# A hybrid decoder layer on one core: the first residual add through a re-ordered copy of the input, VectorE transposes and GpSimd adds

## The chip, the core and the metric

The kernel runs on one core of a Trainium2 chip. The metric is the device time of one execution in microseconds (us). The engines of the core are TensorE (PE in the profile, with its weight loads as PEld), VectorE (DVE), ScalarE (ACT), GpSimd (POOL) and SyncE (SP), which here only issues transfers. The transfers run on 16 DMA engines.

## What is computed

One layer of a decoder on 1024 prompt tokens and 8 sample tokens, with D_MODEL = 1024, all in float32. The core of the reference:

```python
h = rmsnorm(x, w['norm1_w'])
proj = h @ w['w_in']                 # 6672 columns for two head groups
...                                  # group A: 8 HGRN2 heads; group B: 16 Mamba-2 heads
x = x + jnp.concatenate([o_a, y], axis=-1) @ w['w_out']      # first residual
h = rmsnorm(x, w['norm2_w'])
gate, val = jnp.split(h @ w['w_up'], 2, axis=-1)
gate, buf_f_new = causal_dwconv(gate, buf_f, w['ffn_conv_w'], w['ffn_conv_b'])
x = x + (jax.nn.silu(gate) * val) @ w['w_down']
y = rmsnorm(x, final_norm_w)
```

It also returns the new states of both head groups and of the convolutions. The change concerns the term `x +` of the first residual.

## The kernel before, in words

**Layout.** Activations are kept transposed: features on the 128 partitions, tokens along the free dimension, 1024 prompt tokens and then the 8 samples (NT = 1032). The 1024 features are 8 row blocks (KT = 8, index m). Each float32 product is made of three matmuls of split operands: high by high, high by low, low by high.

**Stages.** The input is loaded token by token, normalized and transposed (`first_norm`, L106). Then the columns of w_in are worked off, 128 at a time (`in_job`, L290), with the SSM scan (`ssd`, L715) and the eight HGRN2 heads (`head`, L823) laid between them. The output projection follows in jobs of two row blocks (`out_job`, L1028): first the half of w_out that belongs to the SSM heads (r0 = 8 and 12), then the half of the HGRN heads (r0 = 0 and 4). Then come the second norm, the up projection (`ups`, L1341) and the down projection (`down`, L1399), and the final norm.

**The order of the work.** PE's instructions are in a schedule written by hand (L1107): the jobs' matmuls are a list of steps, `drive` (L266) takes a share of steps for each piece of a scan or head, and `spread` (L240) and `after` (L229) hang small pieces of other work on the count of steps. The other engines' instructions have no such fixed order: a scheduler places each of them on its engine's queue as its inputs, buffers and priority allow. `fetch` (L172) ties a load to the last weight load; a plain `SP.dma_start` isn't tied. Each engine works off its queue in order, SP too: a transfer that waits for a buffer holds up those behind it. Transfers on SP's queue share eight completion semaphores in turn, so each waits until the eighth before it is done.

**The first residual.** For a job with r0 = 8, `out_job` calls `residual_load` (L769) for its two row blocks: for block m it loads the input's columns of that block as xs, two tiles of [128 tokens x 4, 128 features] each holding 512 tokens, in pieces of 512 bytes, and the samples as xd. xs comes from the tag "d" with four buffers, which the broadcast values vb of the heads (L843) use too. After the matmuls ACT copies the sums to x (L1052), and `residual` (L779) is spread over the following steps, 8 apart: PE transposes xs in blocks of 128x128 against the identity into a PSUM bank xtp (L787), DVE adds the bank to x (L782); the samples go through a small transpose xtd (L791). Since x is kept in two halves of 516 tokens, the second 512 prompt tokens are added in pieces of 4 and 508 columns. Later jobs (r0 = 12, 0, 4) add their sums to x on DVE (L1054). Other lines that the prediction names: the split of the mixed activations `ml` (L1012), the scale steps of a head (L866, L867, L872), the masks (L891), the weight split `wl` (L192), the state update `Sh` (L846 to L849), and, in the SSM scan, ecs (L576), S (L581, L582), Cb (L644), Sd (L638 to L643), csb (L543).

Of the kernel before, what the change touches and what calls it, by code (L numbers as in the profile page):

```python
# [8 lines left out]
F32 = mybir.dt.float32  # L9
# [3 lines left out]
ALU = mybir.AluOpType  # L13
# [3 lines left out]
P = 128  # L17
DM = 1024
T = 1024
ND = 8  # L20
# [3 lines left out]
KT = DM // P  # L24
# [26 lines left out]
def hybrid_layer(  # L51
# [9 lines left out]
    V, A, G, PE, SP = nc.vector, nc.scalar, nc.gpsimd, nc.tensor, nc.sync  # L61
# [5 lines left out]
    dram = ctx.enter_context(tc.tile_pool(name="dscr", bufs=1, space=DRAM))  # L67
# [3 lines left out]
    def nm(s):  # L71
        cnt[0] += 1
        return f"{s}_{cnt[0]}"
# [8 lines left out]
    def tl(tag, name, dt=F32):  # L82
        w, n = TAGS[tag]
        return (work if tag in ("hT", "big", "e", "g") else tmp).tile([P, w], dt, tag=tag, bufs=n, name=nm(name))
# [4 lines left out]
    def bank(s, tag="mx"):  # L89
        return psmx.tile([P, 512], F32, tag=tag, bufs=NBANK[tag], name=nm(s))  # L90
# [65 lines left out]
    ident = keep.tile([P, P], F32, name="ident")  # L156
# [15 lines left out]
    def fetch(dst, src):  # L172

        with tc.issue_after(last_w[0].ins):
            SP.dma_start(dst, src)
# [50 lines left out]
    def job(name, load, run):  # L226
        jobs.append((name, load, run))

    def after(n, work):  # L229

        later.append([n, work])
# [8 lines left out]
    def spread(pieces, n, then=None):  # L240

        def go():
            if next(pieces, 0) is None:
                after(n, go)
            elif then is not None:
                then()
        go()
# [72 lines left out]
    def conv_state(src2d, nrow, ntile, out):  # L320
        def rows(j0):
            rt = half("rt")
            nj = min(4, ntile - j0)
            fetch(rt[:nrow, :nj * P], src2d[:, j0 * P:(j0 + nj) * P])
            return rt, nj

        nxt = rows(0)
        for j0 in range(0, ntile, 4):
            yield
            (rt, nj), nxt = nxt, rows(j0 + 4) if j0 + 4 < ntile else None  # L330
            ps = bank("cst", "nx")
            for j in range(nj):
                PE.transpose(ps[:, j * nrow:(j + 1) * nrow], rt[:nrow, j * P:(j + 1) * P], ident[:nrow, :nrow])
            V.tensor_copy(out[:, j0:j0 + nj, :], ps[:, :nj * nrow].rearrange("p (j r) -> p j r", r=nrow))
# [92 lines left out]
    for c, cs in enumerate(chunks):  # L427
        ps = psmm.tile([P, 512], F32, tag="mm", name=nm("dt"))
# [273 lines left out]
    def ssm_conv_state():  # L702
        for j0 in range(0, XT, 4):
            yield
            ps = bank("l11", "nx")
            for j in range(4):
                PE.transpose(ps[:11, j * P:(j + 1) * P], last11[:, j0 + j, :], ident)
            csr = keep.tile([16, 512], F32, tag="csr", bufs=1, name=nm("csr"))
            V.tensor_copy(csr[:11, :512], ps[:11, :])
            cl = slice(j0 * P, (j0 + 4) * P)  # L710
            SP.dma_start(cs_prompt[0, 0, :, cl], csr[0:3, :512])
            SP.dma_start(cs_sample[0, :, 2, cl], csr[3:11, :512])
        SP.dma_start(cs_sample[0, :, 0:2, :], state_conv_ssm[0, :, 1:3, :])
# [16 lines left out]
    def once(work):  # L730
        def run():
            work()
            return
            yield
        return run
# [30 lines left out]

    blk = [slice(i * P, (i + 1) * P) for i in range(4)]

    def residual_load(m):  # L769
        ms = slice(m * P, (m + 1) * P)  # L770
        xs = [tl("d", "xs")[:, :512] for _ in range(2)]
        xd = small.tile([ND, P], F32, tag="xd", name=nm("xd"))
        for i in range(2):
            fetch(xs[i].rearrange("p (i m) -> p i m", m=P),
                  x_prompt[0, i * 512:(i + 1) * 512, ms].rearrange("(i p) m -> p i m", p=P))
        fetch(xd, x_sample[:, 0, ms])
        return xs, xd

    def residual(out, xs, xd):  # L779

        def add(x_, ps):
            V.tensor_tensor(x_, x_, ps, op=ALU.add)  # L782

        for i0 in range(2):
            ps = bank("xtp")
            for i in range(4):
                PE.transpose(ps[:, blk[i]], xs[i0][:, blk[i]], ident)  # L787
            if i0 == 0:
                add(out[0][:, 0:512], ps)
                ps = bank("xtd", "nx")  # L790
                PE.transpose(ps[:, :ND], xd, ident[:ND, :ND])  # L791
                add(out[1][:, 508:516], ps[:, :ND])
            else:
                add(out[0][:, 512:516], ps[:, 0:4])
                add(out[1][:, 0:508], ps[:, 4:512])
            yield

    xh = [[None] * KT for _ in range(2)]
# [1 line left out]
    def head_in(h):  # L800
        t = {}

        def f_end():
            f, k = t["f"], tl("big", "k")
            A.activation(f[:, :NT], f[:, :NT], AF.Identity, bias=lbt[:, 0, h:h + 1], scale=lbt[:, 1, h:h + 1])
            V.tensor_scalar(k[:, :NT], f[:, :NT], -1.0, 1.0, op0=ALU.mult, op1=ALU.add)
            t["k"] = k

        for n, off, func in (("f", OFF_F, AF.Sigmoid), ("q", OFF_Q, AF.Silu), ("v", OFF_I, AF.Copy),
                             ("sg", OFF_G, AF.Silu)):  # L810
            def evict(c, cs, ps, n=n, func=func):
                A.activation(t[n][:, cs], ps, func)

            def begin(n=n):
                t[n] = tl("e" if h == 0 and n == "f" else "big", n)

            if h == H - 1 and n == "sg":
                in_job_last(f"{n}{h}", off + h * P, evict, begin)
            else:
                in_job(f"{n}{h}", off + h * P, evict, begin, f_end if n == "f" else None)  # L820
        return t
# [206 lines left out]
    def out_job(r0, m, halves=(0, 1), last=False):  # L1028
        def load():
            w = wload(w_out[0, r0 * P:(r0 + 4) * P, m * P:(m + 2) * P], 4, 2 * P,  # L1030
                      kept=(r0 // 4 * 4 + m // 2, halves[0]) if len(halves) == 1 else None)
            return w, [residual_load(m + i) for i in range(2)] if r0 == 8 else None
# [52 lines left out]
    def conv_states():  # L1085
        yield from ssm_conv_state()
        yield from conv_state(state_conv_ffn[0].rearrange("b r d -> (b r) d"), 16, FT, fbufT)
        yield
# [3 lines left out]
    heads[0] = head_in(0)  # L1092
    ssm_gate(1)
    heads[1] = head_in(1)
    job("conv", None, once(lambda: spread(conv_states(), 60)))
    for h in range(2, H):
        heads[h] = head_in(h)

# [256 lines left out]
    with tc.manual_schedule(engines={mybir.EngineType.PE}):  # L1355
# [43 lines left out]
        def down(w, kt, msl, acts, c):  # L1399
            q = quarters[c]  # L1400
            ps = psmm.tile([P, 512], F32, tag="mm", name=nm("dn"))[:, :q.stop - q.start]
            for k in range(kt):
                hi, lo = acts[k]
                wh, wl = w(k)
                mm(ps, wh[:, msl], hi[:, q], start=(k == 0), stop=False)
                mm(ps, wh[:, msl], lo[:, q], start=False, stop=False)
                mm(ps, wl[:, msl], hi[:, q], start=False, stop=(k == kt - 1))
                tick()
            return ps

        acts = [act_load(k) for k in range(RND)]
        for r0 in range(0, FT - RND, RND):
# [3 lines left out]
            for m in range(0, KT, 2):  # L1416
                wh, wl = wload(w_down[0, rows, m * P:(m + 2) * P], nk, 2 * P)
                for i in range(2):
# [3 lines left out]
                    for c, cs in enumerate(quarters):  # L1422
                        ps = down(lambda k: (wh[:, k, :], wl[:, k, :]), nk, slice(i * P, (i + 1) * P), acts, c)
# [14 lines left out]
    for c in (3, 0, 1, 2):  # L1438
        cs = quarters[c]
        for m in range(KT):  # L1440
            ps = down(lambda k: wd[k], nk, slice(m * P, (m + 1) * P), acts, c)
# [52 lines left out]
```

## Time and profile before

| | |
|---|---|
| three timed runs | 1771.92, 1772.98, 1773.81 us; median 1772.98 |
| the profiled execution | the page gives its span, 1770.0 us; no other time of it is given |
| ACT busy, DVE busy, POOL busy over the span | 822.8, 1121.0, 476.3 us |
| granted TensorE clock, mean | 0.996 |
| DMA | 190.76 MB in 220325 packets, 13644 of them under 512 bytes |
| PE transposes of the residual (xtp) | 64, first at 835.0 us, last at 925.5 us |
| loads of xs | 16 of 256 KB, first issued at 783.0 us, last at 911.9 us |

A line of a timeline has the start in us, the duration, the engine, the line of the kernel, the operation, the output and inputs by name, and the shape; "x4" joins four instructions in a row, and a bracket gives the time that the engine sat idle before it and what ended that. Matmuls overlap, so the distance of their starts says more than their durations. A line of a group has the count, the busy time in us and the mean in ns, and then the idle time before them. The column "PEclk" is the TensorE clock that was granted, as a share of the full one.

### The profile page before, as it was taken

To read this page: it belongs to the slowest core of one execution; us is meant where nothing else is said; L and a number is where in the kernel's file an instruction comes from. 1 tells how busy PE (TensorE), PEld (TensorE's weight loads), DVE (VectorE), ACT (ScalarE), POOL (GpSimd) and SP (SyncE) were. 2 spreads that over 40 slices of the span, in tenths; PEclk is the share of its full clock that TensorE was granted. 3 is DMA by queue.
4 is the path that set the end of the run, shared out by engine and by line. 5 is a ranking of instruction groups with operands and counts; after the bars stand their busy time and mean duration, and the time that the engine had idled before them with its cause. 6 is when DMAs were issued, how large, how long until landed. Compare 5 with 4: busy or idle time off the path is not lost. (4 is left out here: it accounts for less than half of the span.)

```text
span 1770.0 us, 38596 instructions
## 1 busy us (share of the span) xinstructions
PE 1720.0 (97%) x16143; PEld 1672.4 (94%) x16143; DVE 1121.0 (63%) x2021; ACT 822.8 (46%) x1472; POOL 476.3 (27%) x477
## 2 busy tenths in 40 slices
PE   7999899999999999999999999999999999999997
PEld 6998798999999999999899989999999999999997
DVE  6667966565554564567746688776666767444545
ACT  7677688454544555455423374343333434111114
POOL 2103331120110110111100355666666664000002
PEclk9999999999999999999999999999999999999999
DMA  4144635542222221234336742222222225422212
GB/s 155 40 127 126 183 99 149 177 136 96 75 83 58 85 75 51 77 97 139 115 108 204 243 128 73 72 84 83 86 73 73 82 82 213 152 85 78 92 61 97
DMA packets 220325, 190.76 MB, mean 108 GB/s; under 512 B 13644, under 2 KB 195414, under 8 KB 220134
## 3 DMA queue, kind: packets, MB, share of 16 engines
q1 hardware_dynamic: 219862, 188.19, 34.0%
q8 instruction: 127, 2.08, 0.5%
q14 instruction: 48, 0.39, 0.1%
q0 software_dynamic: 288, 0.10, 0.0%
HBM read 145.72 MB, written 42.71 MB: 106 GB/s over the span
## 5 line engine op out<-in xcount | busy, mean ns | idle before, releaser
L93 PE MATMUL mm<-hh,wh 128*128 128x344 f32 x1248 | 406.9, 327 | 0.6 <-ACT sz L672 0.6
L93 PE MATMUL mm<-hl,wh 128*128 128x344 f32 x1248 | 406.0, 326 | 0.0
L93 PE MATMUL mm<-hh,wl 128*128 128x344 f32 x1248 | 403.7, 324 | 0.0
L93 PEld LDWEIGHTS mm<-hh,wh 128*128 128x128 f32 x1248 | 236.4, 190 | 4.2 <-issue 2.0
L93 PEld LDWEIGHTS mm<-hl,wh 128*128 128x128 f32 x1248 | 236.6, 190 | 2.4 <-issue 0.9
L93 PEld LDWEIGHTS mm<-hh,wl 128*128 128x128 f32 x1248 | 236.5, 190 | 2.0 <-issue 1.2
L190 ACT CAST wh<-ws 128x1024 fp32r<-128x1024 f32 x96 | 100.5, 1047 | 237.4 <-PE dn L93 135.5
L93 PE MATMUL ub<-uh,wh 128*128 128x258 f32 x704 | 199.3, 283 | 3.1 <-DVE fext L1307 2.7
L93 PE MATMUL ub<-ul,wh 128*128 128x258 f32 x704 | 199.0, 283 | 0.0
L93 PE MATMUL ub<-uh,wl 128*128 128x258 f32 x704 | 198.7, 282 | 0.0
L93 PE MATMUL dn<-ah,wh 128*128 128x256 f32 (+1 forms) x640 | 181.2, 283 | 2.1 <-DVE x L1424 2.1
L93 PE MATMUL dn<-al,wh 128*128 128x256 f32 (+1 forms) x640 | 180.6, 282 | 0.0
L93 PE MATMUL dn<-ah,wl 128*128 128x256 f32 (+1 forms) x640 | 180.1, 281 | 0.0
L192 DVE TENSOR_TENSOR wl<-ws,wh 128x1024 fp32r<-128x1024 f32 x88 | 115.6, 1313 | 72.1 <-ACT wh L190 71.1
L93 PE MATMUL ua<-uh,wh 128*128 128x258 f32 x528 | 149.6, 283 | 1.9 <-DVE val L1319 1.2
L93 PE MATMUL mm<-mh,wh 128*128 128x258 f32 x512 | 146.5, 286 | 3.5 <-DVE x L1054 2.1
L93 PE MATMUL ua<-ul,wh 128*128 128x258 f32 x528 | 149.3, 283 | 0.0
L93 PE MATMUL ua<-uh,wl 128*128 128x258 f32 x528 | 148.3, 281 | 0.0
L93 PE MATMUL mm<-mh,wl 128*128 128x258 f32 x512 | 145.0, 283 | 0.9 <-issue 0.9
L93 PE MATMUL mm<-ml,wh 128*128 128x258 f32 x512 | 145.1, 283 | 0.7 <-DVE ml L1012 0.7
L93 PEld LDWEIGHTS ub<-uh,wh 128*128 128x128 f32 x704 | 132.9, 189 | 3.7 <-DVE fext L1307 2.9
L1257 DVE TENSOR_TENSOR wl<-wt,wh 128x512 fp32r<-128x512 f32 x88 | 90.1, 1043 | 70.0 <-ACT wh L1256 69.7
(355 smaller groups left out, 4070.0 us busy)
## 6 DMA issues: line engine op xcount, KB each, us to landing
ws<-in_w_in_dram SPq DMA_DIRECT2D x52, 512.0 KB
ws<-in_w_up_dram SPq DMA_DIRECT2D x44, 512.0 KB
ws<-in_w_out_dram SPq DMA_DIRECT2D x24, 512.0 KB
act_d<-val SPq DMA_DIRECT2D x22, 516.0 KB
al<-act_d SPq DMA_DIRECT2D x22, 516.0 KB
ws<-in_w_down_dram SPq DMA_DIRECT2D x22, 512.0 KB
ml<-mix_d SPq DMA_DIRECT2D x48, 172.0 KB
csb<-cs_d SPq DMA_DIRECT2D x32, 256.0 KB
```

What stands on the lines that cost most here:

```text
L93: PE.matmul(out, lhsT, rhs, start=start, stop=stop)
L190: A.copy(wh[:, :n], ws[:, :n])
L192: V.tensor_tensor(wl[:, :n], ws[:, :n], wh[:, :n].bitcast(F32), op=ALU.subtract)
L1257: V.tensor_tensor(lo[:, cs], sums[name], hi[:, cs].bitcast(F32), op=ALU.subtract)
```

## The change

The input is first copied within memory to a scratch tensor `xb_d` in which each block of 32 tokens by 32 features stands so that a transpose within 32x32 blocks gives the wanted layout: row 32a + j, columns 32b to 32b + 31 of xb_d[m] hold the 32 features of column group a of block m for the token 32b + j. 32 transfers make this copy, each with 1024 pieces of 128 bytes. They are issued by `token_blocks`, started after the convolution states and spread 40 steps apart. `residual_load` then reads whole rows of xb_d. In `residual`, DVE transposes xs in place, 128x512 at once and block by block, and POOL adds the result to x; PE's transposes of xs and the PSUM bank are gone. The samples keep PE's small transpose and DVE's add.

```diff
+    xb_d = dram.tile([KT, P, T], F32, name="xb_d")
+
+    def token_blocks():
+        for m in range(KT):
+            for a in range(4):
+                f0 = m * P + 32 * a
+                SP.dma_start(xb_d[m, 32 * a:32 * a + 32].rearrange("j (b i) -> j b i", i=32),
+                             x_prompt[0, :, f0:f0 + 32].rearrange("(b j) i -> j b i", j=32))
+                yield
+
     def residual_load(m):
...
         for i in range(2):
-            fetch(xs[i].rearrange("p (i m) -> p i m", m=P),
-                  x_prompt[0, i * 512:(i + 1) * 512, ms].rearrange("(i p) m -> p i m", p=P))
+            fetch(xs[i], xb_d[m][:, i * 512:(i + 1) * 512])
         fetch(xd, x_sample[:, 0, ms])
         return xs, xd
 
     def residual(out, xs, xd):
 
-        def add(x_, ps):
-            V.tensor_tensor(x_, x_, ps, op=ALU.add)
+        def add(x_, y_):
+            G.tensor_tensor(x_, x_, y_, op=ALU.add)
 
         for i0 in range(2):
-            ps = bank("xtp")
-            for i in range(4):
-                PE.transpose(ps[:, blk[i]], xs[i0][:, blk[i]], ident)
+            V.transpose(xs[i0], xs[i0])
             if i0 == 0:
-                add(out[0][:, 0:512], ps)
+                add(out[0][:, 0:512], xs[0])
                 ps = bank("xtd", "nx")
                 PE.transpose(ps[:, :ND], xd, ident[:ND, :ND])
-                add(out[1][:, 508:516], ps[:, :ND])
+                V.tensor_tensor(out[1][:, 508:516], out[1][:, 508:516], ps[:, :ND], op=ALU.add)
             else:
-                add(out[0][:, 512:516], ps[:, 0:4])
-                add(out[1][:, 0:508], ps[:, 4:512])
+                add(out[0][:, 512:516], xs[1][:, 0:4])
+                add(out[1][:, 0:508], xs[1][:, 4:512])
             yield
...
-    job("conv", None, once(lambda: spread(conv_states(), 60)))
+    job("conv", None, once(lambda: spread(conv_states(), 60, lambda: spread(token_blocks(), 40))))
```

## The prediction, made before the change was run

> **What bounds the kernel now.** I read the page first, then the busy time by stage, then who waits for whom.
>
> ```profile
> span 1770.0 us, 38596 instructions
> PE 1720.0 (97%) x16143; PEld 1672.4 (94%) x16143; DVE 1121.0 (63%) x2021; ACT 822.8 (46%) x1472; POOL 476.3 (27%) x477
> ```
>
> TensorE (PE) is busy 97% of the span, so a microsecond counts only if it is taken from PE or from a wait of PE. The next view gives the busy time of each engine in chosen stages (columns: stage, its length, PE, PEld, DVE, ACT, POOL, granted clock, DMA share, GB/s):
>
> ```profile
> 150.00:230.00 80.00, 70.51 (x481) 64.53 (x480) 69.60 (x117) 54.88 (x117) 26.72 (x24) 0.98 0.61 172
> 820.00:840.00 20.00, 19.00 (x376) 18.08 (x376) 19.76 (x38) 12.87 (x28) 3.86 (x3) 1.00 0.47 157
> 840.00:860.00 20.00, 17.18 (x298) 15.66 (x297) 17.82 (x31) 11.47 (x27) 4.61 (x4) 1.00 0.66 193
> 860.00:926.00 66.00, 65.75 (x544) 64.43 (x543) 29.73 (x65) 19.46 (x38) 2.85 (x2) 1.00 0.26 81
> ```
>
> Three places matter. From 860 to 926 us PE is full and DVE is half empty: PE binds. From 820 to 860 PE loses 1.00 + 2.82 us and DVE is busy 37.6 of 40: there DVE binds nearly as much as PE. From 150 to 230 us, far ahead of the residual, PE loses 9.5 us while DVE is at 87% and DMA at 0.61: a stage of short chains with no slack. Its largest waits of PE, and those of ACT behind transfers there (total, times, longest), are:
>
> ```profile
> PE xp L554 <- DVE ecs L576: 2.9, 2, 2.7
> PE yo L93 <- DVE S L582: 2.6, 1, 2.6
> PE sT L607 <- POOL Cb L644: 2.1, 1, 2.1
> ACT Sd L640 <- DMA Sd<-in_state_ssm_dram: 11.2, 4, 6.4
> ACT csb L543 <- DMA csb<-cs_d: 7.8, 4, 3.6
> ```
>
> **What leaves PE.** The order of PE's instructions is written by hand, and in the changed program it is the old one without 64 transposes of 128x128 (L787). What one costs is read from starts, not from durations, because matmuls overlap:
>
> ```profile
> 902.55 0.28 PE L93 MATMUL mm<-mh,wl 128*128 128x258 f32 x1
> 902.67 0.60 PE L787 MATMUL xtp<-ident,xs 128*128 128x128 f32 x4
> 903.20 0.22 PE L791 MATMUL xtd<-ident,xd 8*128 8x8 f32 x1
> 903.36 0.39 PE L93 MATMUL mm<-mh,wh 128*128 128x258 f32 x1
> ...
> 904.43 0.60 PE L787 MATMUL xtp<-ident,xs 128*128 128x128 f32 x4
> 904.79 0.37 PE L93 MATMUL mm<-mh,wl 128*128 128x258 f32 x1
> 904.99 0.28 PE L93 MATMUL mm<-mh,wh 128*128 128x258 f32 x1
> ```
>
> A matmul of this stream starts every 0.12 us (902.55 to 902.67). The second group of four delays its successor by 0.36 us, and the successor then takes 0.20 instead of 0.12 to the next start: 0.44 us. The first group takes 0.53 us to the start of the small transpose xtd, which stays; some of that is xtd's own start, so 0.36 to 0.53. I take 0.45 for each of the 16 groups: 7.2 us, between 6.4 and 7.8. Ten groups stand after 860 us, where PE binds: 4.5 us gained in full. Six stand between 835 and 860, where DVE is late too: of their 2.7 us I count 1.5. **PE: -6.0 us.**
>
> **What changes on DVE.** It loses 24 adds and gains 16 transposes of 128x512 in place:
>
> ```profile
> L782 DVE TENSOR_TENSOR x<-x,xtp 128x512 f32<-128x512 f32 x8 | 5.5, 684 | 22.9 <-PE xtp L787 22.9
> L782 DVE TENSOR_TENSOR x<-x,xtp 128x508 f32<-128x508 f32 x8 | 5.4, 675 | 0.0
> L782 DVE TENSOR_TENSOR x<-x,xtp 128x4 f32<-128x4 f32 x8 | 1.2, 153 | 3.2 <-PE xtp L787 3.1
> L609 DVE COPY so<-sT 128x512 f32<-128x512 f32 x2 | 1.4, 676 | 0.0
> L806 DVE TENSOR_SCALAR k<-f 128x1032 f32<-128x1032 f32 x8 | 5.6, 695 | 3.4 <-ACT f L805 3.4
> ```
>
> The adds are 12.1 us. No row shows a DVE transpose. The nearest is the copy of 128x512 at 0.68; L806 does 1032 elements in 0.695, so 0.35 us is the low end, and four passes of the copy, 2.7 us, the high one. I take 0.68: 16 x 0.68 = 10.9 us, 1.2 less than the adds. [...] The first four transposes also move: in the changed program they stand behind a COPY_PREDICATED that ends a busy stretch, and DVE sits idle right there:
>
> ```profile
> 788.72 0.44 DVE L891 COPY_PREDICATED amc<-mlow,a 128x256 f32<-128x256 uint8 x1
> 793.84 1.23 DVE L192 TENSOR_TENSOR wl<-ws,wh 128x1024 fp32r<-128x1024 f32 x1 [4.69 <-ACT wh L190]
> ```
>
> The 4.69 us cover those four (2.7 us) if xs has landed, so 820 to 860 is relieved of the adds of the first two row blocks, some 3 us. At 2.7 us each the cover would be gone, and 6 us of them would stand before wl.
>
> **What comes to POOL, and back to DVE.** POOL gets 16 large adds and 8 of four columns. This stretch shows what a POOL add does to DVE (POOL first, then DVE):
>
> ```profile
> 839.26 1.04 POOL L846 TENSOR_TENSOR vb<-vb,k 128x512 f32<-128x512 f32 x1 [12.57 <-DMA vb<-vd_d]
> 840.38 1.44 POOL L848 TENSOR_TENSOR Sh<-Sh,vb 128x512 f32<-128x512 f32 x1
> 841.78 1.31 POOL L846 TENSOR_TENSOR vb<-vb,k 128x512 f32<-128x512 f32 x1
> 843.17 1.60 POOL L848 TENSOR_TENSOR Sh<-Sh,vb 128x512 f32<-128x512 f32 x1
> ```
>
> ```profile
> 837.80 0.94 DVE L1012 TENSOR_TENSOR ml<-ml,mh 128x344 fp32r<-128x344 f32 x2
> 839.32 2.88 DVE L1012 TENSOR_TENSOR ml<-ml,mh 128x344 fp32r<-128x344 f32 x2
> 842.45 1.19 DVE L866 TENSOR_TENSOR f<-f,tt 128x512 f32<-128x512 f32 x1
> 843.57 1.76 DVE L867 TENSOR_TENSOR q<-q,tt 128x512 f32<-128x512 f32 x1
> 845.25 0.68 DVE L866 TENSOR_TENSOR k<-f,tt 128x512 f32<-128x512 f32 x1
> ```
>
> Two ml take 0.94 alone and 2.88 beside POOL; f and q take 1.19 and 1.76 instead of 0.68. Four POOL instructions cost DVE 1.94 + 0.51 + 1.08 = 3.5 us, 0.9 each. The 16 new adds may cost DVE up to 14 us. Ten of them fall behind 860, where DVE has 36 us to spare: nothing. Six fall before, up to 5.3 us, against the 3 us that left. The rest, 2.3 us, is DVE's at worst; I count 1.0 as reaching PE. Bounds: -2 (DVE's relief counts) to +4.
>
> The buffers of xs are now freed by POOL's add instead of PE's transpose, and vb uses the same four. On SP's queue vb (row 839.26 waited for it) and what is queued behind it, the write of Sh and the loads of ml, start later by about one POOL add and one transpose, some 2 us. Its consumer on PE comes much later:
>
> ```profile
> 856.68 0.64 PE L93 MATMUL od<-Sh,qb 128*32 128x128 f32 x16
> ```
>
> Sh is ready at 844.8, so 12 us cover it. No charge; if the cover failed, 2 us. The copy from PSUM by ACT ahead of the add is unchanged, and the next reader of x is the job after.
>
> **What the re-ordering costs.** 32 transfers, memory to memory, each 128 KB in 1024 pieces of 128 bytes. The call spreads them over the steps of PE's order, but nothing ties them to it: in the changed program 20 stand on SP's queue up to just behind this weight load, and the last 12 among the loads of the stage from 120 to 230 us.
>
> ```profile
> 110.39 0.38 SPq L189 DMA_DIRECT2D ws<-in_w_in_dram  x1
> ```
>
> Two windows give prices for small pieces, 0.4 us of 64-byte pieces (16.6 to 17.0) and 1.0 us of 512-byte pieces (91 to 92), both into SBUF:
>
> ```profile
> DMA packets 693, 0.07 MB, mean 180 GB/s; under 512 B 686, under 2 KB 686, under 8 KB 693
> ...
> DMA packets 689, 0.34 MB, mean 344 GB/s; under 512 B 19, under 2 KB 689, under 8 KB 689
> ```
>
> With 16 DMA engines that is 9 ns and 23 ns of an engine for a piece. 128 bytes lie between: 64 pieces per engine make 0.6 to 1.5 us for a transfer. Writing to memory in such pieces is in no row; if it doubles the price, 3 us. I take 1 us: 32 us of the DMA engines in all. Up to 150 us PE has no wait to lengthen. In 150 to 230 the 12 transfers add 12 us to 49 us of DMA work; most stand ahead of ecs loads, which are asked for long before use. I charge **+1.0 us**, between -3 (the loads and DVE's instructions stand in another order here, and the S chain, 2.6 us of wait, may be freed) and +10 (rival 3). The reloads of xs come in 2 KB rows instead of 512-byte pieces: no charge, none waits for PE now.
>
> **Sum.** -6.0 (PE) + 1.0 (DVE beside POOL) + 1.0 (transfers) = -4.0. Behind 926 us everything follows PE, so it is carried to the end: span 1766.0. The page's execution is given by its span alone; the three runs have a median of 1772.98, 2.98 above it, for what lies around the span. **Forecast 1769.0 us.** About 0.2% (3.5 us) is what a measurement of this kernel can tell from no change.
>
> **Rivals.**
> 1. *All of PE's time comes back*: DVE's relief before 860 covers POOL's blocking and the new order frees a wait of the 150 to 230 stage: -7.2 - 2.5, about 1763. For it: DVE's idle 4.69 us. Against: 2.88 beside 0.94. Chance 0.23.
> 2. *The gain is eaten before 860*: the six early groups give nothing (-4.5), POOL's adds cost PE 3 us, transfers 1: about 1772.5. For it: DVE at 37.6 of 40. Chance 0.24.
> 3. *Slower*: the 12 transfers of the 150 to 230 stage take 3 us each or more, 36 us on top of 49 in 80: the loads of Sd and csb, already waited for by ACT for 11.2 and 7.8 us, come 1 to 3 us later each time, and PE's 9.5 us of wait doubles: -5 + 10, about 1778. It decides from some 2.5 us a transfer on. For it: no row shows a write to memory in such small pieces. Against: the 64-byte row. Chance 0.15. [...]
> 4. *DVE's transposes run at four passes*, 2.7 us: 32 us more on DVE, most of it in its spare time, some 7 us of it before 860: about 1776. Chance 0.06.
>
> **How the numbers follow.** Forecast 0.32 (1766 to 1771), rivals 0.23, 0.24, 0.15, 0.06. The bound for faster, 1769.4, cuts the forecast's case in about 0.27 and 0.05. Faster: 0.27 + 0.23 = 0.50; within 0.2%: 0.05 + 0.24 and a little of 4, 0.30; slower: 0.20. The range leaves out half of rival 3 above and the best of rival 1 below: 1761 to 1778.
>
> **What would show it.** PE's starts around xtd 0.12 apart and about 64 instructions fewer; DVE transposes of 0.6 to 0.7 us in the gap at 789; POOL adds of 1.0 to 1.6 us from 836 on, with DVE rows beside them stretched; PE's busy time in 150 to 230 near 70 of 80. It is wrong if transposes or the 128-byte transfers are far dearer than their nearest rows, or if PE's wait before 860 grows by more than 3 us.

## The result and the profile after

| | median, us | runs | ratio to before, 95% interval |
|---|---|---|---|
| before, in the same sessions | 1773.69 | 15 | |
| changed kernel | 1769.21 | 15 | 0.9971 [0.9961, 0.9980] |

The change makes the kernel faster by 0.29%, which is 5.1 us of 1773.7 (3.5 to 6.9). The forecast of 1769.0 us, a gain of 4.0, is met to 0.2 us in the time. The experiments below show that this is partly luck: two terms of the sum were off by some 5 us each, in opposite directions.

The page of the changed kernel, first lines:

```profile
span 1769.2 us, 38520 instructions
PE 1717.5 (97%) x16079; PEld 1669.4 (94%) x16079; DVE 1123.7 (64%) x2013; ACT 824.7 (47%) x1474; POOL 503.6 (28%) x501
```

PE has 64 instructions fewer and POOL 24 more, as planned. This profiled execution took 1770.87 us, 1.7 more than its span. The prediction had put 2.98 us around the span, from the page's span and another execution's time. So the two spans shown, 1770.0 and 1769.2, differ by less than the medians: the profiled execution of before lies 2.0 us below its median of 1773.69 (1770.0 + 1.7), and that of the changed kernel 1.7 above its own.

Busy time by stage in the changed kernel (columns as in the prediction: stage, length, PE, PEld, DVE, ACT, POOL, granted clock, DMA share, GB/s):

```profile
150.00:230.00 80.00, 74.25 (x506) 67.48 (x503) 68.69 (x112) 55.48 (x115) 27.04 (x22) 0.98 0.69 179
...
820.00:840.00 20.00, 17.64 (x360) 16.66 (x359) 19.86 (x32) 9.84 (x21) 9.15 (x8) 0.91 0.40 125
840.00:860.00 20.00, 12.72 (x262) 11.48 (x260) 19.92 (x30) 11.36 (x27) 9.86 (x8) 0.99 0.66 191
```

Against the same rows of before: PE gains 3.7 us in 150 to 230, where nothing of the residual runs. In 820 to 860 it falls from 36.2 to 30.4 of 40 us, DVE is full (39.8 of 40), and POOL's work has more than doubled.

Since PE's order is the same in both kernels apart from what was removed, the traces can be compared instruction by instruction. For each PE instruction that both have, take its start in the changed kernel minus its start in the kernel before; the change of this lag over a stage is what the stage lost (+) or gained (-). This table is worked out from PE's rows; the stages are in the time of before.

| kernel | to 140 us | 140–290 | 290–825 | 825–870 | 870–926 | 926–1190 | to the end |
|---|---|---|---|---|---|---|---|
| changed kernel | +1.3 | -4.2 | 0.0 | +6.6 | -3.5 | +0.9 | -1.6 |
| e1_copies_only | 0.0 | -4.1 | -1.4 | +3.1 | 0.0 | -0.4 | -0.3 |
| e2_adds_dve | +0.8 | -5.6 | +0.4 | +4.2 | -3.5 | +0.5 | -1.6 |
| e3_tied | +4.2 | +1.4 | -1.2 | +4.6 | -3.5 | +1.2 | -0.1 |
| e4_no_residual | +1.2 | +0.9 | -2.0 | -1.7 | -3.5 | +0.7 | +0.5 |
| e5_xtd_mx | +0.2 | -4.8 | +0.6 | -0.7 | -3.5 | -1.4 | -1.6 |
| e6_poolq | +0.2 | -4.5 | +3.4 | +8.1 | -2.0 | +1.1 | -1.1 |
| e7_dve_mx | +4.1 | -4.8 | 0.0 | +1.0 | -3.5 | +0.7 | -1.5 |
| e8_half_copies | +4.2 | -0.3 | -3.2 | +3.4 | 0.0 | +0.5 | -0.2 |
| e9_before_mx | +0.1 | -1.0 | -1.0 | +2.3 | 0.0 | +0.6 | +1.0 |
| e10_warm | +0.7 | -4.9 | -0.3 | +4.9 | -3.5 | +1.1 | -1.6 |
| e11_m1_dve | +0.6 | -4.8 | +0.1 | -1.0 | -3.5 | +0.3 | -1.6 |

Each row is one execution, and the first column (0 to +4.2, ahead of any residual) shows what chance alone does: the three values above 4 (e3, e7 and e8: +4.2, +4.1, +4.2) come with a dip of the clock to half near 40 us in these executions. Three stages carry the story: 140–290, 825–870 and 870–926.

What PE and then DVE did in 825 to 870 of the changed kernel. The waits of PE between 828 and 872 us (total, times, longest):

```profile
PE xtd L798 <- DVE odr L944: 4.2, 1, 4.2
PE mm L93 <- DVE ml L1019: 1.7, 1, 1.7
PE mm L93 <- ACT x L1059: 1.6, 2, 1.1
PE a L93 <- DVE v L874: 1.3, 1, 1.3
```

The longest is new: xtd and od share the one bank of the tag "nx", so the small transpose of the samples cannot start before DVE has copied od out (odr). In before that wait was 0.42 us. PE's rows around it:

```profile
855.18 0.64 PE L93 MATMUL od<-Sh,qb 128*32 128x128 f32 x16
860.03 0.27 PE L798 MATMUL xtd<-ident,xd 8*128 8x8 f32 x1 [4.21 <-DVE odr L944]
860.24 0.58 PE L93 MATMUL mm<-mh,wh 128*128 128x258 f32 x1
860.62 0.42 PE L93 MATMUL mm<-ml,wh 128*128 128x258 f32 x1
860.83 0.42 PE L93 MATMUL mm<-mh,wl 128*128 128x258 f32 x1
```

Behind the wait the same matmuls start 0.21 us apart instead of 0.12: the granted clock is half (0.50 from 860 to 864 us). Over 860 to 880 the mean is 0.84:

```profile
860.00:880.00 20.00, 19.84 (x142) 19.47 (x143) 7.87 (x20) 5.20 (x11) 3.51 (x3) 0.84 0.20 62
```

0.16 of 20 us is 3.2 us of PE's work. The wait of 4.2 us thus cost about 7.

Why odr is late: DVE's rows, and below them POOL's of the same time.

```profile
829.81 1.58 DVE L1019 TENSOR_TENSOR ml<-ml,mh 128x344 fp32r<-128x344 f32 x1
...
841.84 1.75 DVE L874 TENSOR_TENSOR q<-q,tt 128x512 f32<-128x512 f32 x1
843.52 1.77 DVE L873 TENSOR_TENSOR k<-f,tt 128x512 f32<-128x512 f32 x1
845.21 0.68 DVE L874 TENSOR_TENSOR v<-q,tt 128x512 f32<-128x512 f32 x1
...
846.77 2.42 DVE L1019 TENSOR_TENSOR ml<-ml,mh 128x344 fp32r<-128x344 f32 x3
...
854.25 2.96 DVE L1019 TENSOR_TENSOR ml<-ml,mh 128x344 fp32r<-128x344 f32 x5
857.13 1.47 DVE L794 STREAM_TRANSPOSE xs<-xs 128x512 f32<-128x512 f32 x2
858.52 0.65 DVE L873 TENSOR_TENSOR f<-f,tt 128x512 f32<-128x512 f32 x1
859.10 0.68 DVE L874 TENSOR_TENSOR q<-q,tt 128x512 f32<-128x512 f32 x1
859.70 0.28 DVE L944 COPY odr<-od 128x128 f32<-128x128 f32 x1
```

```profile
829.00 2.45 POOL L791 TENSOR_TENSOR x<-x,xs 128x512 f32<-128x512 f32 x2 [5.15 <-ACT x L1059]
...
841.45 1.61 POOL L855 TENSOR_TENSOR Sh<-Sh,vb 128x512 f32<-128x512 f32 x1
843.01 2.34 POOL L791 TENSOR_TENSOR x<-x,xs 128x512 f32<-128x512 f32 x2
847.02 1.37 POOL L791 TENSOR_TENSOR x<-x,xs 128x508 f32<-128x508 f32 x1 [1.67 <-ACT x L1059]
```

k takes 1.77 beside an add of POOL, and v, right behind it without one, 0.68: 1.09 more. (q's 1.75 stands beside POOL's update of Sh, not beside an add of the residual; in the kernel before it takes 1.76 there too.) The three ml take 2.42. In the kernel before POOL rested there:

```profile
846.79 1.35 DVE L1012 TENSOR_TENSOR ml<-ml,mh 128x344 fp32r<-128x344 f32 x3
```

That is 1.07 less. The stretched rows are not all: right ahead of f, q and odr DVE runs two of its new transposes, 1.47 us. In the kernel before odr came at

```profile
858.00 0.28 DVE L937 COPY odr<-od 128x128 f32<-128x128 f32 x1
```

although there PE's od came 1.5 us later (856.68). How much of the 4.2 us is due to POOL's adds and how much to these transposes, no run here separates fully: with the adds on DVE (e2) 1.7 us of the wait are left.

### The profile page after: what moved, and what is told of

It is laid out like the page before. It is cut to its first block, busy times and chain, and to the rows that moved or that the text cites. A ratio compares the mean times of both kernels' runs of the same rounds, so it can differ in the third digit from the quotient of the medians.

```text
span 1769.2 us, 38520 instructions
## 1 busy us (share of the span) xinstructions
PE 1717.5 (97%) x16079; PEld 1669.4 (94%) x16079; DVE 1123.7 (64%) x2013; ACT 824.7 (47%) x1474; POOL 503.6 (28%) x501
```

## The experiments

Times are given by the ratio to the kernel before in the same session. "us" after a ratio is that share of some 1774 us.

**e1_copies_only.** The kernel before plus `token_blocks` and the call that starts it; `residual_load` and `residual` as before.

```diff
+    xb_d = dram.tile([KT, P, T], F32, name="xb_d")
+    def token_blocks():
...
-    job("conv", None, once(lambda: spread(conv_states(), 60)))
+    job("conv", None, once(lambda: spread(conv_states(), 60, lambda: spread(token_blocks(), 40))))
```

> The kernel before with the 32 transfers added and nothing else: PE's transposes and DVE's adds of the residual stay, and nothing reads the copy. Up to the first residual every engine has the instructions of the changed kernel in the changed kernel's order. Theory A (the transfers' gain is the new order of the stage from 120 to 230 us, in which the page of the changed kernel shows PE busy 74.3 of 80 instead of 70.5): 2 to 4 us below the kernel before, about 1770.5, with PE's busy time in that stage near 74. Theory B (the step of the prediction: the transfers cost about 1 us): 1 us above the kernel before, about 1774.5. Theory C (that stage of the one profiled execution was chance): within 1 us of the kernel before, and the stage at 70 to 74 by chance.

Measured: 0.9982 [0.9970, 0.9994], 3.2 us faster (1.1 to 5.3). Theory A. The stage of 150 to 230:

```profile
150.00:230.00 80.00, 74.05 (x506) 67.74 (x505) 69.46 (x114) 56.60 (x117) 25.19 (x21) 0.98 0.68 176
```

32 transfers that nobody reads make the kernel faster. Up to the residual this program has the changed kernel's order on every engine. The scheduler, which places DVE's, ACT's, POOL's and SP's instructions, has chosen another order for the SSM scan once these transfers are there.

**e8_half_copies.** e1 with half of each transfer. With these, DVE, ACT and POOL keep the order of the kernel before.

```diff
-                SP.dma_start(xb_d[m, 32 * a:32 * a + 32].rearrange("j (b i) -> j b i", i=32),
-                             x_prompt[0, :, f0:f0 + 32].rearrange("(b j) i -> j b i", j=32))
+                SP.dma_start(xb_d[m, 32 * a:32 * a + 32, 0:512].rearrange("j (b i) -> j b i", i=32),
+                             x_prompt[0, 0:512, f0:f0 + 32].rearrange("(b j) i -> j b i", j=32))
```

> The kernel before with 32 transfers of half the size each (512 pieces of 128 bytes, the first 512 tokens), which nothing reads. With these DVE, ACT and POOL keep exactly the order of the kernel before. Theory A (the 3 us of the first experiment come from the new order of instructions): within 1 us of the kernel before. Theory B (they come from the transfers themselves or where they stand on SP's queue): 2 to 3 us below it. By the prediction's price, 1 us for a full transfer: up to 0.5 us above it.

Measured: 0.9993 [0.9981, 1.0005], between 3.4 us faster and 0.9 slower, the middle 1.2 us faster, just outside theory A's 1 us; its interval reaches theory B's 2 to 3. The lag table separates them better: 140–290 gives 0.3 us here and 4.1 to 5.6 in every kernel with the new order. This execution has one dip of the clock more there than that of before, some 1.7 us (granted clock 0.96 from 150 to 230, in before 0.98). Counted with one dip each, e8 gains 2.0 us, e9, which adds no transfer, 2.7, and the kernels with the new order 3.1 to 4.9: still apart, but less clearly. The busy time of PE would mislead:

```profile
150.00:230.00 80.00, 73.42 (x497) 66.08 (x496) 71.69 (x122) 53.94 (x114) 28.71 (x25) 0.96 0.63 171
```

73.42 is close to e1's, but at a granted clock of 0.96 instead of 0.98 and with 497 matmuls instead of 506: at the slower clock PE was nearly as busy and did less.

**e3_tied.** The changed kernel with the transfers tied to the last weight load.

```diff
-                SP.dma_start(xb_d[m, 32 * a:32 * a + 32].rearrange("j (b i) -> j b i", i=32),
-                             x_prompt[0, :, f0:f0 + 32].rearrange("(b j) i -> j b i", j=32))
+                fetch(xb_d[m, 32 * a:32 * a + 32].rearrange("j (b i) -> j b i", i=32),
+                      x_prompt[0, :, f0:f0 + 32].rearrange("(b j) i -> j b i", j=32))
```

> The changed kernel with each of the 32 transfers tied to the last weight load, as the other loads are: they then stand on SP's queue one by one from about 370 to 800 us, and up to there all engines have the order of the kernel before. Theory A (the untied transfers bring an order of the stage of 120 to 230 us that is worth 3 us): the gain goes, about 1772, PE's busy time in 150 to 230 back near 70.5. Theory B (that stage was chance, or the transfers cost there): 1768 to 1769, or less. The stage of 820 to 860 should be as in the changed kernel by both.

Measured: 0.9995 [0.9980, 1.0010], 0.9 us faster (between 3.5 faster and 1.8 slower). Theory A: the gain of the early stage is gone.

```profile
150.00:230.00 80.00, 70.39 (x484) 63.40 (x483) 68.82 (x117) 51.45 (x110) 28.52 (x24) 0.98 0.60 165
```

With before, e1 and the changed kernel this makes a table of two by two: old order and old residual 0; new order alone -3.2; new residual alone -0.9; both -5.1. So by the middle values most of what the change as a whole gained is the order of a stage that it does not mean to touch. The entry of the new residual alone is the least sure of them. What the order frees is seen in PE's waits between 150 and 230 of the changed kernel:

```profile
PE yo L93 <- DVE S L582: 3.1, 1, 3.1
...
PE xp L554 <- DVE ecs L576: 0.3, 1, 0.3
```

ecs had cost 2.9 us, and Cb (2.1 us in before) is no longer in the list; S stays (2.6 in before).

**e4_no_residual.** The kernel before without the residual of the prompt tokens: `x +` is left out for the 1024 prompt tokens, the samples keep theirs. No transfers are added.

```diff
-        for i in range(2):
-            fetch(xs[i].rearrange("p (i m) -> p i m", m=P),
-                  x_prompt[0, i * 512:(i + 1) * 512, ms].rearrange("(i p) m -> p i m", p=P))
...
-        for i0 in range(2):
-            ps = bank("xtp")
-            for i in range(4):
-                PE.transpose(ps[:, blk[i]], xs[i0][:, blk[i]], ident)
...
+        ps = bank("xtd", "nx")
+        PE.transpose(ps[:, :ND], xd, ident[:ND, :ND])
+        add(out[1][:, 508:516], ps[:, :ND])
```

> The kernel before without the residual of the prompt tokens: no loads of xs, no transposes, no adds of them (the samples keep theirs), and no transfers. It leaves out x + for the 1024 prompt tokens. It is the ceiling of what moving the residual off PE can give with the early order of the kernel before. Theory A (behind 860 us PE's time comes back in full and in 820 to 860 POOL and DVE take away nearly as much as PE gives there): 8 to 11 us below the kernel before, about 1764, some 5 us below the changed kernel. Theory B (820 to 860 loses nothing to the residual; the changed kernel has already all there is): 4 to 6 us below the kernel before, about 1769.

Measured: 0.9954 [0.9940, 0.9968], 8.2 us faster (5.7 to 10.6). Theory A, at its edge. With the old order the residual's whole removal from PE, DVE and SP is worth 8.2 us; the changed kernel's residual gets 0.9 of them (e3).

**e2_adds_dve.** The changed kernel with the prompt's adds on DVE.

```diff
-            G.tensor_tensor(x_, x_, y_, op=ALU.add)
+            V.tensor_tensor(x_, x_, y_, op=ALU.add)
```

> The changed kernel with the 24 adds of the prompt's residual on DVE instead of POOL, both inputs in SBUF; DVE's transposes and the transfers stay, and up to the first residual nothing differs. Theory A (in 820 to 860 us each POOL add holds up DVE by more than the 0.7 us that the same add takes on DVE): PE's busy time of 820 to 860 rises from 30.4 by 2 us or more, and the time is 1 to 3 us below the changed kernel, about 1767. Theory B (DVE is the bound there, and its own 24 adds, six of them before 860, cost more than POOL's beside it): 1 to 3 us above the changed kernel, about 1771. Theory C (the loss there comes from vb, Sh and ml that start late behind xs's buffers on SP's queue): no change, 1769, with PE's busy time there still near 30.

Measured: 0.9949 [0.9932, 0.9965], 9.0 us faster than before (6.2 to 12.1), 3.9 better than the changed kernel; the two intervals overlap by a hair. That is theory A's time, but the stage of 825 to 870 shows only 2.4 us of it (+4.2 instead of +6.6), and PE's busy time of 820 to 860 rises by 1.9 us, just short of the 2 expected. In these two executions most of the rest lies in 140–290, where both kernels have the same order. DVE's rows for the scale step that took 1.75 and 1.77 above:

```profile
835.78 0.69 DVE L874 TENSOR_TENSOR q<-q,tt 128x512 f32<-128x512 f32 x1
836.38 0.69 DVE L873 TENSOR_TENSOR k<-f,tt 128x512 f32<-128x512 f32 x1
```

POOL worked beside them, and this time POOL's row is the stretched one (1.04 us in the kernel before):

```profile
836.04 2.53 POOL L853 TENSOR_TENSOR vb<-vb,k 128x512 f32<-128x512 f32 x1 [13.87 <-DMA vb<-vd_d]
```

But PE's waits between 828 and 872 have not gone, they have changed places:

```profile
PE mm L93 <- ACT x L1059: 5.1, 1, 5.1
PE xtd L798 <- DVE odr L944: 1.7, 1, 1.7
```

ACT in turn stands for ml: in that stage its queue has

```profile
ACT mh L1018 <- DMA ml<-mix_d: 10.8, 5, 6.2
```

and the loads of the longest of these waits stand on SP's queue behind both writes of Sh, which wait for POOL. SP's waits between 836 and 846, and the loads:

```profile
SPq L856 <- POOL Sh L855: 6.3, 2, 5.2
...
843.01 0.39 SPq L856 DMA_DIRECT2D out_dram<-Sh  x1
...
845.77 2.43 SPq L175 DMA_DIRECT2D ml<-mix_d  x5
```

In the changed kernel three loads of ml go out between the two writes (839.50 us). So what held the loads is the order on SP's queue and POOL's late Sh. It is not the prediction's chain of an add that holds a load of xs: SP does wait 11.5 us for DVE's adds to free xs, but from 849 us on, behind this wait.

**e5_xtd_mx.** The changed kernel with xtd in one of the four rotating banks.

```diff
-                ps = bank("xtd", "nx")
+                ps = bank("xtd")
```

> The changed kernel with the samples' small transpose xtd in one of the four rotating PSUM banks instead of the single bank that it shares with od. Nothing else moves but two rows of DVE. In the profiled run of the changed kernel PE stands 4.2 us at xtd, until DVE has copied od out of that bank (odr), and then has half the clock for 6.8 us. Theory A (this wait and the slow clock behind it are most of what 820 to 870 loses): the wait of xtd goes and the time falls by 3 to 6 us below the changed kernel, 8 to 11 below the kernel before, about 1764. Theory B (DVE is late with everything there, and PE stands at the next scale step or at ml instead): within 1 us of the changed kernel, 5 below the kernel before.

Measured: 0.9927 [0.9910, 0.9943], 13.0 us faster than before (10.1 to 16.0), 7.8 better than the changed kernel with intervals well apart, and more than theory A's range. The adds are still on POOL and DVE's rows are as stretched as before, and odr is copied at 858.4. Now nobody waits for it. PE's waits between 825 and 875:

```profile
PE mm L93 <- ACT x L1059: 1.8, 1, 1.8
PE mm L93 <- DVE ml L1019: 1.7, 1, 1.7
PE a L93 <- DVE v L874: 1.3, 1, 1.3
```

**e9_before_mx.** The same edit in the kernel before.

> The kernel before with xtd in a rotating PSUM bank, as in the fifth experiment, and nothing else (two rows of DVE change places). Theory A (the shared bank costs only where DVE is late with odr; the profile of the kernel before shows 0.4 us of wait there): within 1 us of the kernel before. Theory B (the bank is worth as much without the change, and the gain of the fifth experiment has nothing to do with it): 5 to 8 us below the kernel before.

Measured: 1.0001 [0.9990, 1.0012]. Theory A: the shared bank is harmless until DVE is late, and it is the change that makes DVE late.

**e7_dve_mx.** Both edits, adds on DVE and xtd in a rotating bank.

> The changed kernel with the adds of the prompt's residual on DVE, as in the second experiment, and xtd in a rotating PSUM bank. Theory A (POOL's blocking and the shared bank are two separate losses): below either alone, 10 to 12 us below the kernel before, about 1761. Theory B (with the adds on DVE, odr is in time and the bank costs little; its profile shows 1.7 us of wait at xtd): 8 to 10 us below the kernel before, as in the second experiment.

Measured: 0.9940 [0.9924, 0.9956], 10.6 us faster than before (7.8 to 13.5). By the middle value this is theory A's lower edge and 1.6 beyond e2, but 2.3 short of e5: the losses do not add up. With the bank out of the way POOL's adds are no worse than DVE's, within the intervals: the order that comes with the adds on DVE brings the 5-us wait behind ml's loads again (5.2 us in its profile, ACT's for ml 10.5, SP's for POOL's Sh 5.2).

**e10_warm.** The changed kernel with 40 transposes of the identity right before the third row block's xtd. They add work to PE and nothing to the result.

```diff
...
+                if m == 2:
+                    dm = bank("dm")
+                    for i in range(40):
+                        PE.transpose(dm[:, blk[i % 4]], ident, ident)
                 ps = bank("xtd", "nx")
```

> The changed kernel with 40 more transposes of the identity on PE, into a bank that nothing reads, right before the small transpose xtd of the third row block, where PE stands 4.2 us for odr in the profiled run. They fill the wait; the computation is unchanged. Theory A (the idle 4.2 us bring the half clock of 6.8 us behind them, 3.4 us of PE's work): the wait for odr stays, the half clock behind it goes, 2 to 4 us below the changed kernel, 7 to 9 below the kernel before. Theory B (the half clock has another cause): no change, or up to 2 us slower by the added work, 3 to 5 below the kernel before.

Measured: 0.9959 [0.9947, 0.9972], 7.3 us faster than before (5.0 to 9.4). That is 2.2 us below the changed kernel by the middle values, but the intervals overlap, so the time alone does not settle it. The rows do:

```profile
853.01 0.65 PE L93 MATMUL od<-Sh,qb 128*32 128x128 f32 x16
853.59 4.59 PE L800 MATMUL dm<-ident 128*128 128x128 f32 x40
858.10 0.22 PE L802 MATMUL xtd<-ident,xd 8*128 8x8 f32 x1
...
858.48 0.28 PE L93 MATMUL mm<-ml,wh 128*128 128x258 f32 x1
858.60 0.28 PE L93 MATMUL mm<-mh,wl 128*128 128x258 f32 x1
```

```profile
860.00:880.00 20.00, 18.47 (x156) 18.12 (x155) 10.61 (x26) 7.39 (x14) 2.70 (x3) 1.00 0.19 57
```

xtd comes just as late behind od, but the matmuls after it start 0.12 us apart at once, and the clock of 860 to 880 is 1.00 instead of 0.84. Here, then, the half clock came from PE's wait of 4.2 us. The lag of 825–870 falls by 1.7 us only (+4.9 instead of +6.6): a new wait of PE a little later, 1.5 us for DVE's add of the samples, takes back part of what the clock gives.

**e6_poolq.** The changed kernel with the loads of xs issued by POOL.

```diff
-            fetch(xs[i], xb_d[m][:, i * 512:(i + 1) * 512])
+            with tc.issue_after(last_w[0].ins):
+                G.dma_start(xs[i], xb_d[m][:, i * 512:(i + 1) * 512])
```

> The changed kernel with the 16 loads of xs issued by POOL instead of SP. A load of xs that waits for a buffer then holds up nothing on SP's queue, where the profile of the changed kernel shows waits of 15.5 us for POOL's adds between 820 and 870 and the loads of ml behind them. POOL frees these buffers itself. Theory A (step 4 of the prediction, no charge: late loads there cost PE nothing): within 1 us of the changed kernel, 5 below the kernel before. Theory B (the held-up loads of ml are a good part of the loss in 820 to 870): 2 to 4 us below the changed kernel, 7 to 9 below the kernel before.

Measured: 1.0002 [0.9991, 1.0013]; neither theory. The edit brought a loss of its own, so it says nothing on SP's queue. The scheduler now puts transposes of xs ahead of a mask on DVE, and DVE stands there for their loads:

```profile
777.59 0.71 DVE L795 STREAM_TRANSPOSE xs<-xs 128x512 f32<-128x512 f32 x1 [7.60 <-DMA xs<-xb_d]
```

PE also waited 5.0 us at xtd. What the held-up loads of ml cost in the changed kernel stays open.

**e11_m1_dve.** e5 with the adds of row block 1 on DVE.

```diff
...
-            G.tensor_tensor(x_, x_, y_, op=ALU.add)
+            (V if m == 1 else G).tensor_tensor(x_, x_, y_, op=ALU.add)
...
-                ps = bank("xtd", "nx")
+                ps = bank("xtd")
```

> The fifth experiment's kernel (xtd in a rotating bank) with the adds of row block 1 alone on DVE; the other seven blocks add on POOL. In the fifth experiment's profile these adds (841.7 and 845.7 us) stand beside q and k of 1.75 and 1.77 and ml of 2.40 instead of 0.68, 0.68 and 1.36. Theory A (these stretched rows are PE's waits there, 1.3 for v and 1.7 for ml): 1 to 3 us below the fifth experiment's kernel, some 15 below the kernel before. Theory B (xs's buffers, then freed by DVE, hold up the loads of ml on SP's queue, as in the runs with all adds on DVE, where PE waits 5.1 us): no gain or a loss of up to 3 us, 10 to 13 below the kernel before.

Measured: 0.9921 [0.9909, 0.9934], 14.0 us faster than before (11.7 to 16.1), median 1761.21. It is the quickest version, though e5's interval covers it. Of theory A's two waits one is gone, v's (1.3 to 0.2 us); ml's is still 1.7, and a transpose of kt waits 1.5 us for DVE instead.

## Why the prediction was right, step by step

- **What leaves PE behind 860 us: right.** The lag falls by 3.52 us over the eight groups between 870 and 926, 0.44 a group against the predicted 0.45, and by the same amount in every kernel without PE's transposes, e4 included (only e6, where a dip of the clock falls into the stage, has 2.0).
- **The six groups before 860, -1.5 us: wrong; and POOL beside DVE, +1.0 us: the step that failed.** The price of an add was right: 1.07 and 1.09 us of DVE in the rows above, 0.9 predicted. "I count 1.0 as reaching PE" was wrong. The prediction looked for PE's wait at the scale steps and at ml. There it did grow, by 2.1 us (v 0.2 to 1.3, ml 0.7 to 1.7), but PE stopped longest at xtd, on a bank shared with od that the prediction did not look at, and then ran at half clock (0.50). Together with the two groups at 865.7 and 869.4 the steps gave -1.4 for this stage; the traces show +6.6. The kernel before was itself caught at a good moment there: with the old residual, e1, e8 and e9 lose 2.3 to 3.4 in the same stage. Each has there one wait of PE for ACT's copy of x (3.6, 3.9 and 3.1 us) and behind it a dip of the clock (0.91 from 840 to 860 in e1 and e9); in before's profile the longest such wait is 0.9 us, and the dip is missing (1.00). In e1:

```profile
840.00:860.00 20.00, 15.30 (x263) 14.16 (x249) 13.05 (x28) 9.52 (x24) 0.00 (x0) 0.91 0.52 152
```

  So the change's own loss there is some 3 to 4 us against such an execution, and e5 and e11, which lose nothing, show how much of it the bank was.
- **DVE's transposes: right.** In the changed kernel (minimum, median, maximum in ns):

```profile
L794 DVE STREAM_TRANSPOSE xs<-xs x16: 667/708/712, 785.9 to 917.8; 128x512 f32<-128x512 f32 x16
```

  The median is 0.71 us where 0.68 was taken (four in a row take 2.48, 0.62 each). The first four ran at 785.90 in DVE's idle time, as forecast. But two of them stand right ahead of odr (857.13, 1.47 us), which the prediction did not count.
- **The transfers, +1.0 us: the size was within its range, the sign was wrong.** From 114 to 115 us the DMA engines are full with them (90% busy or more in each of 40 slices):

```profile
DMA packets 1655, 0.22 MB, mean 219 GB/s; under 512 B 1628, under 2 KB 1655, under 8 KB 1655
```

  16 us of engines over 1655 pieces is 9.7 ns a piece, or 0.62 us for a transfer of 1024; 0.6 to 1.5 was the prediction's range and 1 us was taken. Rival 3, which needed 2.5 us, is out. By the same count the prediction read 9 ns for 64 bytes and 23 ns for 512 bytes, both into SBUF, and 9.7 ns for 128 bytes, memory to memory, lies between. What the transfers did to PE was the opposite of a charge, -3.2 us in e1, by the order. The prediction had named that as its lower bound, -3, and charged +1.0.
- **xs's buffers and SP's queue, no charge: right for this kernel.** ACT's waits for ml are 4.3 us in the changed kernel against 5.1 before. SP's queue can cost PE time all the same: with the adds on DVE (e2, e7) these waits reach 10.5 to 10.8 and PE pays 5, there behind POOL's Sh and not behind xs.
- **The sum.** The early order was 4 to 5 us better than charged, the stage of 825 to 870 about 5 worse against such an execution; these cancel. The 2.98 us around the span should have been 1.7. The time was right; the account behind it was right for PE's transposes, DVE's transposes and the transfers' length only.

## What to carry to other kernels

When work moves from PE to DVE and POOL, look at which PSUM banks and buffers the moved work's neighbours share: here a late copy out of a shared bank stopped PE for 4.2 us though the moved work itself had time, and one word (another bank) was worth more than the whole change (7.8 us against 5.1). That wait of PE of 4.2 us cost about 7, since the granted clock over the 20 us behind it was 0.84: look at the clock behind a long wait too. And test any added instructions alone where a scheduler places the rest: the order that they bring can outweigh what they do.

## What the runs showed of the hardware

- **PE's granted clock fell to half for 3.4 or 6.8 us at a time, most often behind a wait of PE.** In the profiled executions of the two kernels every dip before the end lasts 3.413 us, apart from one of 6.827 us; the changed kernel has 20.5 us of them, the kernel before 10.2 (one more, of 7.2 and 7.1 us, lies at the end of each). Ahead of each dip before the end, or reaching into it, stands a wait of PE of 1.7 to 4.2 us. In the other kernels three dips near 40 us (e3, e7, e8) have no such wait: PE was busy there, and their cause is open. Between 825 and 875 us a clock below 1.00 stands beside or behind each of these waits above 3.5 us: 4.2 us in the changed kernel (0.84 over 860 to 880 us), 3.6 in e1 (0.91 over 840 to 860), 5.1 in e2 (0.79) and 5.2 in e7 (0.83) in that same stretch, 4.1 in e3 and 5.0 in e6 (0.97 and 0.92 over 860 to 926). A shorter wait has a dip in one place and not in another: in the kernel before, waits of 2.7, 1.9 and 1.7 us (up to 155.9, 388.3 and 414.6 us) have one up to 2.1 us behind them (157.3, 389.4 and 416.7 us), and waits of 2.6 and 2.7 us (up to 206.9 and 1063.6 us) have none. The wait of 3.1 us for S near 203 us has one in the changed kernel (207.5 us); in e2, which has the same order there, the clock of 150 to 230 us is 1.00. In the changed kernel a wait of 1.7 us for ml stands ahead of the dip at 832.1 us; with the 4.2-us wait filled by useless transposes (e10) the clock of 860 to 880 us stays at 1.00. What decides over the short waits, no run here shows.
- **Beside an add of POOL some DVE rows took about 1.1 us more, and others nothing.** The three ml (POOL's add 1.37 us) and k (two inputs in SBUF) took 1.07 and 1.09 us more. In e2 it was POOL's row that was long: 2.53 us (1.04 in the kernel before) beside q and k of 0.69. The 16 transposes, which have one input, stayed within 0.67 to 0.71 us though POOL ran beside some of them (857.13 us, beside the add of 856.83). What sets these rows apart, no run here shows.
